# Two token mixers written as lists of steps in a two-layer trunk kernel

## The chip, the cores and the metric

The kernel runs on one core of one Trainium2 chip. The metric is device time in microseconds (us) of one execution; three runs of the kernel before are at hand, and one more execution under the profiler. The core's engines work side by side, each through its own queue in order: PE (TensorE, matmuls; PEld are its weight loads), DVE (VectorE), ACT (ScalarE), POOL (GpSimd) and SP (SyncE, which here issues most loads). PE writes its results into PSUM, where the kernel holds eight tiles of 128x512; the rest lives in SBUF.

## What is computed

A batch of one, 256 tokens, width 1024, two layers. Each layer is a half-step feed-forward block, a token mixer and a second half-step feed-forward block; every part has an RMS norm ahead of it, with shift, scale and gate from a conditioning vector `c`. Layer 0 mixes by MoBA attention (with 256 tokens a single causal block, with a relative-position bias), layer 1 by MLA.

```python
def swiglu(h, w_gate, w_up, w_down):
    return (jax.nn.silu(h @ w_gate) * (h @ w_up)) @ w_down
...
for layer in range(DEPTH):
    mods = c_act @ ada_w[layer] + ada_b[layer]
    sh1, sc1, g1, sh2, sc2, g2, sh3, sc3, g3 = jnp.split(mods, 9, axis=-1)
    h = modulate(rms_norm(x, norm_g[layer, 0]), sh1, sc1)
    x = x + 0.5 * g1[:, None, :] * swiglu(h, ffn_w_gate[layer, 0], ffn_w_up[layer, 0], ffn_w_down[layer, 0])
    h = modulate(rms_norm(x, norm_g[layer, 1]), sh2, sc2)
    mix = moba_attention(h, ...) if layer < N_A_LAYERS else mla_attention(h, ..., shared_k, shared_v, positions)
    x = x + g2[:, None, :] * mix
    h = modulate(rms_norm(x, norm_g[layer, 2]), sh3, sc3)
    x = x + 0.5 * g3[:, None, :] * swiglu(h, ffn_w_gate[layer, 1], ffn_w_up[layer, 1], ffn_w_down[layer, 1])
...
def mla_attention(h, w_dq, q_a_norm_g, w_uq, q_g, w_o, k, v, positions):
    q = (rms_norm(h @ w_dq, q_a_norm_g) @ w_uq).reshape(B, S, MLA_HEADS, MLA_QK)
    q = rms_norm(q, q_g)
    q = jnp.concatenate([q[..., :MLA_NOPE], rope(q[..., MLA_NOPE:], positions)], axis=-1)
    o = causal_block_attention(q, k, v, MLA_QK ** -0.5)
    return o.reshape(B, S, MLA_HEADS * MLA_V) @ w_o
```

All arrays are float32. There are 16 heads; in MoBA of width 64, in MLA 96 for queries and keys (64 and a rotated part of 32) and 64 for values. The feed-forward width is 2816.

## The kernel before

Tokens stand in two tiles of 128 (`t` 0 and 1). A float32 product is made of three matmuls: each operand is split into a rounded part `hi` (an ACT copy) and the rest `lo` (a DVE subtraction), and `mm3` (L393 to L397) sums hi x hi, hi x lo and lo x hi into one PSUM bank. Weights come by SP into `raw` tiles (three buffers) in the order in which `wsrcs` lists them, one ahead of their use; `split` makes their parts.

`ffn` (L506) runs four times. It takes the first 512 hidden columns tile by tile (32 triple products of 512 columns), then 18 blocks of 128 hidden rows with both token tiles side by side as a moving operand of 128x2x128 (16 triple products each, gate and up), then two halves of the down product, 22 blocks deep. In the second half tile 0 runs eight blocks ahead of tile 1, so that tile 0's residual (`ry`, `x`), norm and transposes can go on under tile 1's last eight blocks.

The conditioning vectors, 18 of width 1024, are made on DVE: `ada_vec` (L201) takes eight steps, each a 512 KB load into one of three `adaw` buffers and one accumulation into `acc` (one buffer), and then sums over partitions on PE, `adaps`: with transposes and DVE reductions for shifts and scales, with products by ones for gates, whose `acc` is split first. The steps are dealt out by a planner that counts an estimate of PE's time, `clock`: `pe(us)` adds to it, runs what has come due (`later`), and takes one step of the stream whenever `clock` has passed the next mark. The marks are set by `ada_pace(vectors, us)`, which spreads the steps still wanted over that many clock us, 172 for a feed-forward block (90 for the last); `ada_until(vectors)` takes what is left at once. `ffn` calls it after tile 0's last residual and ahead of tile 0's norm. What the planner emits is then put in order by a scheduler that weighs program order against its own estimate of when operands are ready; each engine's final order can be read from the built kernel.

```python
    def pe(us):
        clock[0] += us
        if busy[0]:
            return
        while pend and pend[0][0] <= clock[0]:
            run_next()
        while pace[0] and clock[0] >= pace[1]:
            pace[1] += pace[0]
            ada(1)
```

The mixers are planned by the same clock. `moba` (L817) projects queries and keys of four groups of four heads (`qk`) and values (`vals`); some microseconds of clock later (`T_WAIT`, `S_WAIT`, `PT_WAIT`, `AV_WAIT`) come the transposes `to_T` and the three parts of `attention` (L594): `scores` with the softmax, `transposes` of the weights, `av`. `mla` (L1006) does the same from two latents, normed and transposed by `lat_norm_T`. A query is scaled by its 1/rms (`head_rstd`: ACT square, DVE sums, POOL power) before it is rotated and transposed. `out_proj` (L679) follows, in two halves of the depth, with residual and norm after each tile.

## Time and profile before

| | us |
|---|---|
| runs: lowest, median, highest of 3 | 1061.85, 1062.43, 1064.68 |
| the profiled execution | 1067.16 |
| its span, first to last instruction | 1065.4 |

The profile's lines are read so: engine, operation, `out<-in` with the names of the program's tiles, partitions x elements, how often; then busy us, mean ns of one, and the engine's idle time ahead of them with what ended it. Stages by time: first block to 237 us, MoBA to 372, second block to 557, third to 756, MLA to 874, fourth to the end.

### The profile page before, as it was taken

How to read it: one execution, taken by the hardware profiler on the slowest of the kernel's cores; microseconds unless marked ns; L12 is line 12 of the kernel's file. 1: busy time of each engine (PE TensorE's matmuls, PEld its weight loads, DVE VectorE, ACT ScalarE, POOL GpSimd, SP SyncE). 2: the span in 40 equal slices, each digit the busy share in tenths (PEclk: the TensorE clock that was granted, in tenths of full speed). 3: DMA queues.
4: the chain of work that ended last, by engine and by line, in shares of the span. 5: the costliest groups of instructions: out<-in, count | busy, mean ns of one | idle time of the engine just before them, and what ended most of it. 6: DMA issues, size and time to landing. Idle time of an engine off the chain costs nothing.

```text
span 1065.4 us, 17278 instructions
## 1 busy us (share of the span) xinstructions
PE 1020.8 (96%) x6663; PEld 899.3 (84%) x6663; DVE 810.9 (76%) x1244; ACT 578.6 (54%) x1048; POOL 70.1 (7%) x119
## 2 busy tenths in 40 slices
PE   4999999998999999999999999999988899999998
PEld 2499999886778789999887999988766778999986
DVE  5999977886875789889688888867778758755642
ACT  4364545357675765545348544533868777545531
POOL 4001000002121000000000000000043200000000
PEclk9999999999999999999999999999999999999999
DMA  9999987996845479989897997986354337665450
GB/s 311 322 304 287 376 288 278 335 318 206 310 162 170 139 236 345 337 293 332 295 313 227 328 329 251 318 303 205 117 162 142 119 119 236 223 204 187 161 177 20
DMA packets 166934, 260.65 MB, mean 245 GB/s; under 512 B 8030, under 2 KB 110214, under 8 KB 166852
## 3 DMA queue, kind: packets, MB, share of 16 engines
q1 hardware_dynamic: 164496, 254.70, 70.3%
q0 software_dynamic: 976, 3.37, 1.0%
q10 hardware_dynamic: 1380, 1.49, 0.5%
q8 instruction: 52, 0.85, 0.3%
q14 instruction: 30, 0.25, 0.1%
HBM read 255.33 MB, written 4.19 MB: 244 GB/s over the span
## 4 chain that ended last, share of the span: by engine, by line
PE 77%; DVE 10%; ACT 4%; DMA 4%; POOL 3%; issue 3%; SPq 0%; DVEq 0%; ACTq 0%; POOLq 0%
PE mm L394 23%; PE mm L396 23%; PE mm L395 23%; DVE lo L196 3%; POOL hr L703 3%; DMA adaw<-in_ada_w_dram 2%; PE mm L198 2%; ACT hi L196 1%; DVE oh L722 1%; PE adaps L222 1%; PE at L666 1%; PE at L611 1%; DVE acc L211 1%; DMA raw<-in_ffn_w_gate_dram 1%; ACT y L196 1%
## 5 line engine op out<-in xcount | busy, mean ns | idle before, releaser
L196 DVE TENSOR_TENSOR lo<-raw,hi 128x1024 fp32r<-128x1024 f32 (+2 forms) x316 | 374.3, 1199 | 80.2 <-ACT hi L196 79.3
L196 ACT ACTIVATE hi<-raw 128x1024 fp32r<-128x1024 f32 (+2 forms) x316 | 324.1, 1040 | 171.5 <-PE mm L396 103.6
L394 PE MATMUL mm<-hh,hi 128*128 128x256 f32 x1152 | 328.6, 285 | 0.0
L396 PE MATMUL mm<-hh,lo 128*128 128x256 f32 x1152 | 326.7, 284 | 0.5 <-DVE lo L196 0.5
L395 PE MATMUL mm<-hl,hi 128*128 128x256 f32 x1152 | 326.5, 283 | 0.0
L395 PEld LDWEIGHTS mm<-hl,hi 128*128 128x128 f32 x1152 | 221.7, 192 | 0.6 <-issue 0.2
L396 PEld LDWEIGHTS mm<-hh,lo 128*128 128x128 f32 x1152 | 221.6, 192 | 0.7 <-DVE lo L196 0.7
L394 PEld LDWEIGHTS mm<-hh,hi 128*128 128x128 f32 x1152 | 221.7, 192 | 0.6 <-issue 0.2
L211 DVE SCALAR_TENSOR_TENSOR acc<-adaw,cact,acc 128x1024 f32<-128x1024 f32 x126 | 162.8, 1292 | 20.6 <-DMA adaw<-in_ada_w_dram 16.2
L394 PE MATMUL mm<-hi,gh 128*128 128x512 f32 x352 | 138.0, 392 | 0.0
L395 PE MATMUL mm<-lo,gh 128*128 128x512 f32 x352 | 137.0, 389 | 0.0
L396 PE MATMUL mm<-hi,gl 128*128 128x512 f32 x352 | 137.0, 389 | 0.0
L394 PE MATMUL mm<-hi,hh 128*128 128x512 f32 (+1 forms) x240 | 96.7, 404 | 5.0 <-ACT hh L196 5.0
L396 PE MATMUL mm<-hi,hl 128*128 128x512 f32 (+1 forms) x240 | 94.0, 392 | 1.5 <-DVE hl L196 1.4
L395 PE MATMUL mm<-lo,hh 128*128 128x512 f32 (+1 forms) x240 | 93.4, 390 | 0.0
L560 ACT ACTIVATE g<-mm 128x256 f32<-128x256 f32 x72 | 27.3, 379 | 94.5 <-PE mm L396 94.5
L396 PEld LDWEIGHTS mm<-hi,gl 128*128 128x128 f32 x352 | 66.1, 188 | 13.8
L394 PEld LDWEIGHTS mm<-hi,gh 128*128 128x128 f32 x352 | 66.1, 188 | 13.2
L395 PEld LDWEIGHTS mm<-lo,gh 128*128 128x128 f32 x352 | 66.1, 188 | 13.1
L196 ACT ACTIVATE gh<-g 128x256 fp32r<-128x256 f32 x72 | 29.9, 416 | 69.6 <-DVE g L561 69.6
L394 PEld LDWEIGHTS mm<-hi,hh 128*128 128x128 f32 x240 | 45.1, 188 | 16.1 <-ACT hh L196 7.8
L396 PEld LDWEIGHTS mm<-hi,hl 128*128 128x128 f32 x240 | 45.1, 188 | 13.2 <-DVE hl L196 4.5
(222 smaller groups left out, 1114.8 us busy)
## 6 DMA issues: line engine op xcount, KB each, us to landing
adaw<-in_ada_w_dram SPq DMA_DIRECT2D x144, 512.0 KB, 6.8
raw<-in_ffn_w_gate_dram SPq DMA_DIRECT2D x42, 1024.0 KB, 7.3
raw<-in_ffn_w_up_dram SPq DMA_DIRECT2D x42, 1024.0 KB, 6.9
raw<-in_ffn_w_down_dram SPq DMA_DIRECT2D x40, 1024.0 KB, 6.6
raw<-in_moba_w_qkv_dram SPq DMA_DIRECT2D x16, 512.0 KB, 5.0
adaw<-in_kv_ada_w_dram SPq DMA_DIRECT2D x16, 512.0 KB, 5.6
raw<-in_ffn_w_down_dram SPq DMA_DIRECT2D x8, 512.0 KB, 3.6
raw<-in_moba_w_qkv_dram SPq DMA_DIRECT2D x4, 1024.0 KB
```

The lines of the kernel that those rows point to most:

```text
L196: return fn(*args, **kw)
L198: chain[on] = fn(*args, **kw)
L211: nc.vector.scalar_tensor_tensor(acc, wt, cact[:, k:k + 1], bz if k == 0 else acc, op0=ALU.mult, op1=ALU.add)
L222: nc.tensor.transpose(kslice(pt, j), kslice(acc, 4 * hh + j), ident)
L394: nc.tensor.matmul(ps, lh, rh, start=start, stop=False)
L395: nc.tensor.matmul(ps, lh, rl, start=False, stop=False)
L396: nc.tensor.matmul(ps, ll, rh, start=False, stop=stop)
L560: nc.scalar.activation(g, ps[:, 0], AF.Silu)
L611: nc.tensor.matmul(ps3[:, i, :], qTs(e, t), kTs(e, nk), start=bias is not None, stop=bias is not None or i == len(es) - 1)
L666: nc.tensor.matmul(po[i * DH:(i + 1) * DH, pr, t, :], vs(e, kb), pT[t, e, kb], start=kb == 0, stop=kb == t)
L703: nc.gpsimd.tensor_tensor(r, v2, mhalf[:, :nh], op=ALU.pow)
L722: return fn(*args, **kw)
```

## The change

It writes both mixers as lists of steps. `in_steps` goes through a list and holds each step's matmuls behind the last matmul of the step before in PE's queue, so that within the mixers PE's order is that of the list. The letters: `d`, `e` the two latents, `l`, `c` their transposes, `q`, `k`, `v` the projections, `r`, `u`, `t` transposes of queries and keys, `s`, `p`, `a` scores, transposed weights and values, `o` output products of one tile and one pair of depths, `n` residual and norm of a tile.

In MLA the query is no longer scaled: an ACT copy takes it from PSUM, and its 1/rms scales the maximum and goes into the exponential as a scale per query. The key transposes leave PSUM by DVE in place of ACT. The causal mask is added after the scores and covers only the diagonal block. The output product is split into four pairs of depth for each tile, dealt out among the last attention steps and round the first tile's norm. `mm3` reports another estimate to the planner's clock. Smaller edits: the load order of MoBA's last two projections is swapped, some scratch tiles share a buffer, score tiles have six buffers for five and values three for two, a sum of the head norm is made in place.

```diff
+MOBA_ORDER = ("q00 q01 v00 t0 v010 s0 v011 q100 p0 q101 a0 q11 q20 t1 q210 s1 q211 q300 p1 q301 a1 t2 q310 s2 q311 "
+              "v200 p2 v201 t3 v210 s3 v211 o00 a2 p3 o10 a3 o01 o02 o03 n0 o11 o12 o13 n1").split()
+MLA_ORDER = ("d0 d1 l0 e0 l1 e1 c0 q00 q01 c1 k00 k01 r0 q10 q11 k10 u0 k11 r1 s0 q20 q21 u1 k20 k21 p0 r2 s1 a0 "
+             "q30 q31 u2 k30 k31 p1 r3 s2 a1 u3 o00 s3 o01 p2 o10 a2 p3 o02 a3 o11 o03 n0 o12 o13 n1").split()
...
-                    for g in (0, -1, 1, 2, -2, 3):
+                    for g in (0, -1, 1, 2, 3, -2):
...
-        nc.tensor.matmul(ps, ll, rh, start=False, stop=stop)
-        pe(3 * max(256, rh.shape[-1]) * 0.422e-3)
+        latest[0] = nc.tensor.matmul(ps, ll, rh, start=False, stop=stop)
+        pe(3e-3 * (rh.shape[-1] / 2.4 + 13.3))
+
+    latest = [None]
+    chained = [None]
+
+    def in_steps(order, fns):
+        for w in order:
+            with ExitStack() as es:
+                if chained[0]:
+                    es.enter_context(tc.issue_after(chained[0].ins))
+                latest[0] = None
+                fns[w[0]](*map(int, w[1:]))
+            chained[0] = latest[0] or chained[0]
...
-                if bias is None:
-                    nc.tensor.matmul(ps, ident_b, masks[t], start=True, stop=False)
...
+                if not bias:
+                    latest[0] = nc.tensor.matmul(ps3[:, :, t * P:], ident_b, mask[:, :len(es) * P]
+                                                 .rearrange("p (e k) -> p e k", k=P), start=False, stop=True)
...
+                    raw = small([P, 4], "mxr")[:, :n]
+                    nc.vector.tensor_reduce(raw, ps3, axis=AX.X, op=ALU.max, negate=True)
+                    nc.vector.tensor_tensor(mx, raw, rq(t)[:, es[0]:es[0] + n], op=ALU.mult)
...
-                                         bias=mxs[u][:, i:i + 1], scale=1.0 if bias is None else -1.0,
+                                         bias=mxs[u][:, i:i + 1], scale=-1.0 if bias else rq(t)[:, e:e + 1],
...
+        def products(t, j):
+            for half in range(2):
+                if (t, half) not in acc:
+                    acc[t, half] = mm_tile()
+                for k in (2 * j, 2 * j + 1):
...
+                    mm3(acc[t, half], *hk(oT[t], k), *pls[half, k], start=k == 0, stop=k == KD - 1)
...
-                    r = head_rstd(ap, pq_, GH * QK, QK)
-                    nc.vector.tensor_tensor(qn[:, t], heads(pq_), r[:, :, None].to_broadcast([P, GH, QK]), op=ALU.mult)
...
+                ps = proj(("q", g), t, qlT, QL // P, GH * QK)
+                nc.scalar.activation(qn[g][:, t], heads(ps), AF.Copy)
+                rq[g, t] = head_rstd(ap, ps, GH * QK, QK)
...
-                    nc.scalar.activation(dst[:, :, t * P:(t + 1) * P],
-                                         pt[:QK, :].rearrange("p (e q) -> p e q", q=P), AF.Copy, scale=gcol)
...
+                    if kind == "q":
+                        nc.scalar.activation(*ev, AF.Copy, scale=gcols[0])
+                    else:
+                        nc.vector.tensor_scalar(*ev, gcols[1], None, op0=ALU.mult)
```

## The prediction

> **What bounds the kernel now.** I read the page first, then busy time by stage, then single stretches in order of time.

> ```profile
> span 1065.4 us, 17278 instructions
> PE 1020.8 (96%) x6663; PEld 899.3 (84%) x6663; DVE 810.9 (76%) x1244; ACT 578.6 (54%) x1048; POOL 70.1 (7%) x119
> ```
> ```profile
> 50.00:237.00 187.00, 184.97 (x1462) 169.99 (x1461) 165.84 (x256) 93.29 (x166) 5.85 (x3) 0.99 0.91 311
> 237.00:256.00 19.00, 16.12 (x74) 11.81 (x74) 11.13 (x21) 16.60 (x38) 3.87 (x5) 1.00 0.49 173
> 256.00:363.50 107.50, 104.00 (x582) 86.12 (x581) 78.62 (x160) 67.55 (x135) 16.93 (x10) 1.00 0.63 213
> 363.50:372.00 8.50, 6.37 (x30) 4.33 (x29) 5.70 (x10) 7.88 (x22) 1.12 (x2) 1.00 0.38 125
> 372.00:557.00 185.00, 185.00 (x1243) 170.87 (x1242) 156.81 (x172) 93.42 (x135) 0.00 (x0) 1.00 0.88 305
> 756.00:771.00 15.00, 13.84 (x78) 11.49 (x77) 12.18 (x38) 14.33 (x41) 0.55 (x1) 1.00 0.38 115
> 771.00:867.00 96.00, 85.66 (x531) 69.35 (x531) 73.42 (x169) 66.29 (x164) 25.87 (x20) 1.00 0.44 141
> 867.00:874.00 7.00, 5.32 (x27) 3.89 (x26) 5.66 (x10) 6.58 (x18) 0.82 (x2) 1.00 0.41 126
> ```

> TensorE sets the time. The rows give a stretch, its length, then busy time of PE, PEld, DVE, ACT and POOL. In the second feed-forward block (372 to 557) PE never rests; whatever is taken off DVE or the DMA queues there gains nothing. What a better order can win is PE's rest in the mixers: 3.5 us inside MoBA (256 to 363.5), 10.3 inside MLA (771 to 867), and at their ends 2.9, 2.1, 1.2 and 1.7. The other side of the account is the seam between a feed-forward block and the next norm, where PE has only the rest of tile 1's products as cover.

> **The clock of the plan: the part that decides.** The change also rewrites what `mm3` adds to the planner's clock, from `max(256, n)` columns to `n`, with n the last dimension of the moving operand. For the gate and up products the operand is 128x2x128, so n is 128 while 256 columns move.

> ```profile
> 400.32 0.28 PE L394 MATMUL mm<-hh,hi 128*128 128x256 f32 x1
> 400.44 0.28 PE L395 MATMUL mm<-hl,hi 128*128 128x256 f32 x1
> ```

> Start to start they take 0.12 us, 0.36 for three; the clock was moved 0.324 and is now moved 3e-3 x (128/2.4 + 13.3) = 0.20. The conditioning stream (`ada`, one 512 KB load and one accumulation a step) is paced by that clock: its steps are spread over 172 clock us a block. Up to the call of `ada_until` a block runs 32 triple products of its first columns (not on the clock in the first block), 288 of gate and up, and 80 down products: 0.648 x 112 + 0.324 x 288 = 166 of 172 before, 0.68 x 112 + 0.20 x 288 = 134 now, or 78%; in the first block 112 of 172. The rest of the steps is issued in one go by `ada_until`, at the very end of the block. The order of instructions of the two builds bears this out: after tile 0's last residual is traced, 12, 10 and 8 steps are left at the ends of blocks one, two and three, where before it was 4, none and 1. Each time a whole vector of eight falls behind tile 0's last product. Its column sums (eight transposes, `adaps`) stand in PE's queue *ahead* of the next norm's transposes, so all that follows on PE waits for that vector, though the next norm doesn't use it.

> ```profile
> L211 DVE SCALAR_TENSOR_TENSOR acc<-adaw,cact,acc 128x1024 f32<-128x1024 f32 x126 | 162.8, 1292 | 20.6 <-DMA adaw<-in_ada_w_dram 16.2
> L196 DVE TENSOR_TENSOR lo<-raw,hi 128x1024 fp32r<-128x1024 f32 x300 | 361.5, 1220 | 75.5 <-ACT hi L196 74.7
> L495 DVE TENSOR_TENSOR ry<-mm,gate 128x512 f32<-128x512 f32 x24 | 16.5, 686 | 14.7 <-PE mm L396 14.2
> L496 DVE TENSOR_TENSOR x<-x,ry 128x512 f32<-128x512 f32 x24 | 16.5, 688 | 0.4
> L257 DVE TENSOR_REDUCE acol<-adaps 128x4 f32<-128x512 f32 x12 | 7.8, 684 | 0.8 <-PE adaps L222 0.8
> L196 ACT ACTIVATE y<-tr,m_cols 128x128 f32<-128x128 f32 x80 | 32.6, 457 | 0.2
> L196 ACT ACTIVATE hh<-y 128x256 fp32r<-128x256 f32 x40 | 16.7, 418 | 0.4 <-PE tr L442 0.3
> ```
> ```profile
> 232.37 0.68 DVE L495 TENSOR_TENSOR ry<-mm,gate 128x512 f32<-128x512 f32 x1
> 235.60 0.39 PE L395 MATMUL mm<-lo,gh 128*128 128x512 f32 x1
> 235.83 0.39 PE L396 MATMUL mm<-hi,gl 128*128 128x512 f32 x1
> 236.06 1.03 PE L222 MATMUL adaps<-ident,acc 128*128 128x128 f32 x8
> 236.85 0.48 PE L394 MATMUL mm<-hi,gh 128*128 128x512 f32 x1
> 240.93 0.50 PE L394 MATMUL mm<-hi,hh 128*128 128x512 f32 x1 [0.88 <-ACT hh L196]
> ...
> 554.81 0.68 DVE L495 TENSOR_TENSOR ry<-mm,gate 128x512 f32<-128x512 f32 x1
> 563.35 0.50 PE L394 MATMUL mm<-hi,hh 128*128 128x512 f32 x1 [0.86 <-ACT hh L196]
> ...
> 748.24 0.69 DVE L495 TENSOR_TENSOR ry<-mm,gate 128x512 f32<-128x512 f32 x1 [0.20 <-PE mm L396]
> 756.58 0.45 PE L394 MATMUL mm<-hi,hh 128*128 128x384 f32 x1 [0.47 <-ACT hh L196]
> ```

> Call T the start of tile 0's last residual. From T to the next stage's first product it took 8.56, 8.54 and 8.34 us. Now, from the DVE order of the changed build (each engine works its queue in order, as the rows above show):

> First seam, from T to the end of the vector: nine accumulations 9 x 1.29 = 11.6, the split of the gate sum 1.22, six weight splits 7.3, two residual pairs 2.75, three small ones 0.45 (0.15 each, estimated from their size): T + 23.3. Second seam: `acc` has one buffer, so the vector starts when PE has read the one before it: 18 products at 0.23 (235.60 to 235.83) and eight transposes 0.79 (236.06 to 236.85), T + 4.9; then eight accumulations 10.3, four splits 4.9, a residual pair 1.4, a reduce 0.7, a small one: T + 22.4. Third: T + 4.9, eight accumulations 10.3, splits of 288, 864 and 288 columns (by size 0.35, 1.03, 0.35), pair 1.4, reduce 0.7, 0.15: T + 19.2. Behind that on PE come 0.79 of column sums and a pair of transposes, 0.2, then 2 x 0.457 + 0.418 on ACT, together 2.3. First products: T + 25.6, 24.7, 21.5; extra 17.0, 16.2, 13.2, in sum 46.4.

> To it come the loads. There are three `adaw` buffers, so the fourth load is issued only after the first accumulation.

> ```profile
> DMA to landing us min/median/max: 3.5/6.6/9.2
> ```

> At 3.5 us every load lands before its accumulation is reached; at 6.6 the fourth and seventh are waited for, by my reckoning 2.5, 3.2 and 4.6 us in the three seams. Bounds 46.4 and 56.7; I take 51.5. What is queued behind the waiting instructions on DVE is the next norm's own splits, so nothing passes. On SP the leftover loads wait for their buffers ahead of later weight loads: in the first seam MoBA's value weights are among them, due only after 48 query products (10.9 us), so this costs nothing while those run.

> PE then rests about 15 us at each seam. The nearest row of such a rest is short:

> ```profile
> 90.95 1.63 PE L722 MATMUL tr<-tab,oh 128*128 128x64 bf16 x24 [1.56 <-DVE oh L722]
> ...
> 90.00:95.00 5.00, 4.05 (x37) 3.68 (x38) 5.00 (x13) 3.51 (x18) 0.00 (x0) 0.78 1.13 362
> 95.00:100.00 5.00, 5.00 (x40) 5.00 (x39) 4.87 (x9) 0.62 (x1) 3.23 (x1) 0.88 1.02 373
> ```

> After it the granted clock was 0.78 and 0.88 over two stretches of 5 us: 1.1 + 0.6 = 1.7 us of clock lost. At three seams 5.1; bounds 0 and twice that. Loss in all 56.6.

> **What the mixers win.** The orders written out put 24 products of 512 columns between a query group and its transposes, where before three stood.

> ```profile
> 291.76 0.38 PE L879 MATMUL tr<-ident,qn 128*128 128x128 f32 x2
> 293.45 0.77 PE L879 MATMUL tr<-ident,qn 128*128 128x128 f32 x5 [1.31 <-DVE qn L858]
> ```

> Three such waits make up most of MoBA's rest: gain 4 (0 to 6: a restart costs more than the bar leaves open). In MLA the query's own chain loses the wait for POOL and the scaling on DVE, eight times:

> ```profile
> L703 POOL TENSOR_TENSOR hr<-hv,mhalf 128x4 f32<-128x4 f32 x16 | 22.7, 1420 | 41.8 <-DVE hv L702 41.8
> L1085 DVE TENSOR_TENSOR qn<-mm,hr 128x384 f32<-128x384 f32 x8 | 4.5, 557 | 6.7 <-POOL hr L703 6.7
> L1066 ACT ACTIVATE kT<-tr,gck 96x512 f32<-96x512 f32 x8 | 5.3, 694 | 1.2 <-PE tr L1065 1.2
> L609 PE MATMUL at<-mask,ident_b 128*128 128x512 bf16 x12 | 4.6, 384 | 0.0
> ```

> An ACT copy of 384 columns takes its place (0.5, estimated between the 0.418 for 256 and the 0.694 for 512), and the key transposes' evacuation goes from ACT to DVE, 0.69 each. DVE was busy 73.4 of MLA's 96 us and gives 4.5, takes 5.5: it stays near its load, and three copies of 1/rms ride on the product of four columns. So I don't take all of the 10.3: 8 (0 to 13). The score buffers now hold 1/rms until the exponentials have read it, in eight slots; POOL's next results wait there, which keeps me off the full figure. Masks of 256 for 512 columns in eight of twelve: 8 x 0.11 = 0.9. Output products put round the norm lengthen the cover at the mixers' ends, of 2.1 + 1.7: 2.5. After the long wait at a seam DVE has the splits done that PE waited for in the rows 237:256 and 756:771: 2.5. In the first block DVE was full around 90 us and has fewer accumulations now: 2 of its 2.0 rest and 1.7 clock. Gain in all 19.9. Scratch tiles that now share buffers, the joined masks' set-up and the changed load order of MoBA's last two weights I put at nothing: their users lie a stage apart, and if one waits it is by a split, 1.2.

> PE's bar leaves 10.3 us of rest in MLA. [...]

> Sum: +51.5 + 5.1 - 19.9 = +36.7. On the profiled execution, 1067.16 us with its span of 1065.4, that is 1103.9; the median of the runs is 4.7 lower, 1062.43, so 1099.

> **Rivals.** *The seams cost only what is counted there twice, half.* Were the scheduled splits and residuals hidden behind load waits and the clock not cut, 3 x (10.3 - 2.0 of products) = 25 would be lost and 19.9 won: 1068 to 1080. Against it: the DVE order leaves no idle to hide them in. *The mixers hold more than PE's bars show.* At the second block's share of weight loads (170.87 of 185) MLA's 69.35 would fill 75.1 of its 96 us: 20.9 won in place of 8, 1086. For it speak the many switches between transposes and products, whose pauses a bar covers; against it DVE, busy 73.4 there. *Faster.* If the vectors left over were accumulated under the down products, because their loads come early, the seams cost nothing and 19.9 is won: 1043. It decides where the eight accumulations end before T + 7; that needs `acc` free and eight loads landed with three buffers, against the row of 3.5 us at least. *The queued matmuls don't help.* Waiting at the head of PE's queue, with ACT and DVE each near 75% in MLA, could leave the mixers as they are: +56.6 and 1119.

> **How the numbers follow.** Forecast (1085 to 1112) 0.62; queue without help 0.14; more in the mixers 0.08; half cost 0.08; faster 0.08, of which 0.02 within the bound. A measurement can tell 0.3%, 3.2 us, from no change. So slower 0.92, same 0.02, faster 0.06. The range: low end with 46.4, no clock lost, and gains of 30 (6 + 13 and the ends in full): +16; high end 56.7 + 10.2 less 5: +62. That is 1078 to 1124, which holds the forecast, the larger gain, and most of the queue without help.

> **What would show it.** Right: at three places, about 237, 570 and 780 us, PE rests 10 us or more, its first following instruction is `adaps`, released by DVE `acc`, and the granted clock dips behind each; four to eight accumulations stand in one run on DVE there. Fewer accumulations per us in gate and up stretches, PE still full there. MoBA's waits `tr<-ident,qn` on `qn` gone; MLA's stretch shorter by 5 to 10 us, DVE above 80% busy. Wrong: no rest at the seams, or rests under 5 us; MLA as long as before or longer.

## The result and the profile after

| | before | after |
|---|---|---|
| runs, us: lowest, median, highest | 1061.85, 1063.43, 1064.68 (4) | 1126.91, 1129.07, 1131.39 (4) |
| span of the profiled execution | 1065.4 | 1128.7 |

The changed kernel takes 1.0618 times as long (95% interval 1.0588 to 1.0649), 65.6 us more, where 36.7 were forecast and at most 62 allowed for. The direction was right, the size was not. From the page of the changed kernel: its span, its engines' busy time, the clock that TensorE was granted in 40 slices, and the rows of the accumulations and of the column sums:

```profile
span 1128.7 us, 17306 instructions
PE 1027.2 (91%) x6663; PEld 910.0 (81%) x6663; DVE 821.8 (73%) x1256; ACT 581.3 (52%) x1048; POOL 73.6 (7%) x117
PEclk9999999987999999999987999999798999999999
L214 DVE SCALAR_TENSOR_TENSOR acc<-adaw,cact,acc 128x1024 f32<-128x1024 f32 x126 | 163.0, 1294 | 28.0 <-DMA adaw<-in_ada_w_dram 23.0
...
L225 PE MATMUL adaps<-ident,acc 128*128 128x128 f32 x96 | 15.2, 311 | 52.2 <-DVE acc L214 52.2
```

PE has as many instructions as before and is busy 6.4 us longer, but its share falls from 96% to 91%. The last row holds most of the new rest: 52.2 us ahead of the column sums, all of it waiting for `acc` on DVE. The accumulations themselves stood idle for 28.0 us, 23.0 of them for loads, where it was 20.6 and 16.2. The clock is granted less in and just behind those places: 0.65 over 236 to 265 us, 0.59 over 582 to 607, 0.64 over 796.6 to 815.8.

To see where the rest of the time went, the execution is cut at points that both kernels have: the last product of a feed-forward block, the first product of the next stage, and, behind a mixer, the first two-token product of the feed-forward block (so the mixers' stretches hold its 32 triple products of 512 columns too). The rows give stretch, length, busy time of PE, PEld, DVE, ACT and POOL with instructions, then granted clock, share of the DMA engines and GB/s. First the seams and mixers of before, then of after:

```profile
239.20:240.90 1.70, 0.85 (x6) 0.50 (x4) 1.70 (x3) 1.70 (x6) 0.68 (x2) 1.00 0.96 339
240.90:392.10 151.20, 143.54 (x756) 116.17 (x757) 107.59 (x205) 104.31 (x214) 21.23 (x16) 1.00 0.58 194
561.70:563.40 1.70, 0.84 (x7) 0.51 (x5) 1.70 (x3) 1.70 (x6) 0.00 (x0) 1.00 0.52 172
755.20:756.60 1.40, 0.93 (x8) 0.57 (x6) 1.40 (x4) 1.08 (x4) 0.00 (x0) 1.00 0.57 170
756.60:895.90 139.30, 126.58 (x731) 102.29 (x732) 105.86 (x232) 105.33 (x253) 27.53 (x23) 1.00 0.43 139
```
```profile
241.30:265.10 23.80, 4.07 (x18) 3.27 (x16) 17.87 (x20) 7.67 (x14) 3.06 (x4) 0.57 0.91 306
265.10:413.90 148.80, 143.63 (x756) 117.61 (x757) 105.14 (x199) 102.30 (x211) 21.80 (x13) 0.99 0.59 197
582.20:605.20 23.00, 4.09 (x19) 3.29 (x17) 17.90 (x21) 7.67 (x15) 1.46 (x1) 0.59 0.92 313
796.60:815.80 19.20, 4.06 (x19) 3.32 (x17) 14.90 (x23) 2.72 (x8) 0.70 (x1) 0.64 0.75 240
815.80:959.20 143.40, 126.28 (x731) 106.64 (x732) 108.13 (x238) 104.80 (x250) 23.67 (x22) 0.96 0.38 122
```

The three seams were 1.7, 1.7 and 1.4 us and are 23.8, 23.0 and 19.2: 61.2 more, nearly the whole loss between the profiled executions (1128.7 - 1065.4 = 63.3). MoBA won 2.4. MLA, for which the largest gain was forecast, is 4.1 longer at a granted clock of 0.96. The remaining stretches, all feed-forward, differ by 2.1, -1.3, -0.4 and 0 us.

The second seam in order of time (start, length, engine, line, operation; in brackets the idle time ahead and what ended it):

```profile
575.62 0.69 DVE L512 TENSOR_TENSOR ry<-mm,gate 128x512 f32<-128x512 f32 x1 [1.53 <-PE mm L399]
...
582.08 1.28 DVE L214 SCALAR_TENSOR_TENSOR acc<-adaw,cact,bz 128x1024 f32<-128x1024 f32 x1
...
594.59 2.60 DVE L214 SCALAR_TENSOR_TENSOR acc<-adaw,cact,acc 128x1024 f32<-128x1024 f32 x2
599.84 1.28 DVE L214 SCALAR_TENSOR_TENSOR acc<-adaw,cact,acc 128x1024 f32<-128x1024 f32 x1 [2.66 <-DMA adaw<-in_kv_ada_w_dram]
...
601.18 1.97 PE L225 MATMUL adaps<-ident,acc 128*128 128x128 f32 x8 [18.58 <-DVE acc L214]
602.94 1.91 PE L459 MATMUL tr<-ident,y 128*128 128x128 f32 x8
605.18 0.80 PE L397 MATMUL mm<-hi,hh 128*128 128x512 f32 x1 [0.33 <-ACT hh L199]
```

Tile 0's last residual starts at 575.62, the leftover vector's first accumulation at 582.08. The last accumulation waits 2.66 us for its load, and PE rests 18.6 us until it is done. The norm's transposes stand behind the column sums, and all of it runs at half clock (0.50 over 600 to 606 us): eight column sums take 1.97 us, against 1.03 in the row at 236.06 of before, where the clock was 1.00.

In MLA the first transposes of the query's latent, as PE and DVE show them, and the clock on both sides of that rest:

```profile
826.78 0.34 PE L399 MATMUL mm<-hi,hl 128*128 128x384 f32 x1
831.93 0.90 PE L1013 MATMUL tr<-ident,ly 128*128 128x128 f32 x3 [4.81 <-DVE ly L1007]
832.48 0.59 PE L397 MATMUL mm<-hi,hkv 128*128 128x288 f32 x1
```
```profile
826.00:832.00 6.00, 1.03 (x5) 0.72 (x6) 5.56 (x19) 4.39 (x11) 2.38 (x2) 1.00 0.56 169
832.00:836.00 4.00, 4.00 (x20) 4.00 (x21) 3.33 (x5) 0.49 (x1) 0.00 (x0) 0.58 0.52 144
```

The list has `l0` ahead of `e0`. Its transposes wait 4.8 us for the normed latent `ly`, which DVE (busy 5.56 of these 6 us) makes behind the key latent's modulation, and `e0`'s products are held behind them. After the rest the clock stands at half for most of four us (0.58 over 832 to 836; by its record from 831.96 to 835.37).

### The profile page after: what moved, and what is told of

It reads as the page before. It is cut to its first block, busy times and chain, and to the rows that moved or that the text cites. A ratio compares the mean times of both kernels' runs of the same rounds, so it can differ in the third digit from the quotient of the medians.

```text
span 1128.7 us, 17306 instructions
## 1 busy us (share of the span) xinstructions
PE 1027.2 (91%) x6663; PEld 910.0 (81%) x6663; DVE 821.8 (73%) x1256; ACT 581.3 (52%) x1048; POOL 73.6 (7%) x117
## 4 chain that ended last, share of the span: by engine, by line
PE 68%; DVE 12%; DMA 8%; ACT 5%; issue 4%; SPq 2%; POOL 1%; DVEq 0%; ACTq 0%; POOLq 0%
PE mm L397 21%; PE mm L399 21%; PE mm L398 21%; DMA adaw<-in_ada_w_dram 5%; DVE lo L199 3%; DVE acc L214 3%; DMA adaw<-in_kv_ada_w_dram 2%; SPq L201 2%; ACT hi L199 1%; DMA raw<-in_ffn_w_gate_dram 1%; DVE oh L742 1%; PE adaps L225 1%; ACT s L654 1%; PE at L681 1%; ACT y L199 1%
## 5 line engine op out<-in xcount | busy, mean ns | idle before, releaser
L199 ACT ACTIVATE hi<-raw 128x1024 fp32r<-128x1024 f32 (+2 forms) x316 | 326.3, 1042 | 170.2 <-PE mm L399 103.5
L578 DVE TENSOR_TENSOR g<-mm,g 128x256 f32<-128x256 f32 x72 | 30.2, 419 | 50.3 <-ACT g L577 50.2
L225 PE MATMUL adaps<-ident,acc 128*128 128x128 f32 x96 | 15.2, 311 | 52.2 <-DVE acc L214 52.2
```

The costliest lines, as they stand in the source:

```text
L199: return fn(*args, **kw)
L225: nc.tensor.transpose(kslice(pt, j), kslice(acc, 4 * hh + j), ident)
L578: nc.vector.tensor_tensor(g, ps[:, 1], g, op=ALU.mult)
```

## The experiments

Twelve kernels, each timed beside runs of the kernel before on the same chip (whose medians were 1063.4 to 1066.3 us). MLA's length is that of the stretch above, in one profiled execution of each kernel.

| kernel | median, us | over before (95% interval) | MLA, us |
|---|---|---|---|
| changed | 1129.1 | 1.0618 (1.0588 to 1.0649) | 143.4 |
| changed, all columns counted | 1086.5 | 1.0214 (1.0194 to 1.0234) | 146.6 |
| changed, old estimate | 1074.1 | 1.0097 (1.0080 to 1.0113) | 145.8 |
| before, new estimate | 1122.6 | 1.0549 (1.0533 to 1.0565) | 140.4 |
| changed, leftover after the norm | 1126.4 | 1.0585 (1.0569 to 1.0601) | 158.8 |
| old estimate, not queued | 1060.8 | 0.9958 (0.9937 to 0.9978) | 132.5 |
| old estimate, latents' order | 1069.7 | 1.0038 (1.0021 to 1.0056) | 139.4 |
| old estimate, query scaled | 1090.6 | 1.0232 (1.0206 to 1.0257) | 162.6 |
| changed, late column sums | 1104.3 | 1.0363 (1.0336 to 1.0390) | 146.7 |
| old estimate, not queued, query scaled | 1070.7 | 1.0049 (1.0030 to 1.0067) | 141.4 |
| old estimate, rests filled | 1073.8 | 1.0075 (1.0052 to 1.0097) | 143.5 |
| changed, not queued | 1116.6 | 1.0483 (1.0462 to 1.0505) | 133.2 |
| all columns counted, not queued | 1071.1 | 1.0054 (1.0031 to 1.0077) | 133.3 |

### The estimate: three kernels

```diff
-        pe(3e-3 * (rh.shape[-1] / 2.4 + 13.3))
+        pe(3e-3 * (math.prod(rh.shape[1:]) / 2.4 + 13.3))
```

> The changed kernel with one edit: mm3 tells the planner's clock all columns of the moving operand (256 for 128x2x128, so 0.36 us a triple product), not the last dimension alone. Theory A (the 65.6 us over before are the three seams, 52.7 in the changed profile, and about 7 of clock behind them; the mixers as written neither win nor lose much): 1129 - 52.7 - 7 = about 1069, range 1060 to 1080, no column sum waited for at 237, 570, 780. Theory B (the late seam at the third block's end also causes what MLA lost, because weights and splits come late behind it): the mixers' gains show and the time is 1040 to 1056, below before. Theory C (the pace isn't the cause): 1110 or more.

```diff
-        pe(3e-3 * (rh.shape[-1] / 2.4 + 13.3))
+        pe(3 * max(256, rh.shape[-1]) * 0.422e-3)
```

> The changed kernel with the old estimate in mm3, 3 x max(256, n) x 0.422 ns, so that the conditioning stream is dealt out as before. What is left are the step lists, the 1/rms in the exponential and the output products round the norm. Theory A: within 5 us of the run with all columns counted, 1060 to 1080. Theory B: 1040 to 1056. Theory C: 1110 or more. If this one is more than 8 us faster or slower than the run with all columns, the exact pace matters beyond whether whole vectors are left over.

The third is the kernel before with the new line, the reverse of the second:

> The kernel before with one edit: the new estimate in mm3 (last dimension only). Nothing of the mixers changed but what their planner's clock decides. Theory A: 1063 + 53 + 7 = about 1122, range 1110 to 1132, with the three rests of PE ahead of the column sums. Theory B (the losses in MLA belong to the step lists meeting a late seam): 1110 to 1118, because the old mixers are planned by the same clock and shift. Theory C: 1060 to 1070.

The seams' stretches of that third kernel, in windows like those above:

```profile
237.00:261.00 24.00, 3.68 (x18) 3.06 (x16) 18.13 (x20) 7.64 (x14) 3.06 (x4) 0.64 0.94 330
576.90:600.50 23.60, 4.11 (x18) 3.29 (x17) 18.00 (x21) 7.60 (x15) 1.59 (x2) 0.58 0.89 305
791.50:810.70 19.20, 4.00 (x19) 3.34 (x17) 14.91 (x23) 2.77 (x9) 0.70 (x1) 0.64 0.72 240
```

The one line in the old kernel makes the seams of the changed one, and 1122.6 us were measured for 1122 forecast by theory A; with the line put back, the changed kernel is at 1074.1. So the estimate makes the seams, and theory C falls. Theory B falls too: without the seams the mixers as written don't win, they are 1% slower than before. The first of the three was missed: the true count was to give 1069 and gave 1086.5. It has no rest over 0.2 us ahead of these column sums, but at the second block's end one of 5.7 us ahead of the norm's own transposes:

```profile
571.38 0.69 PE L459 MATMUL tr<-ident,y 128*128 128x128 f32 x2 [5.69 <-ACT y L454]
```

### The leftover steps taken later

```diff
-                    ada_until(ada_to)
+                    pace[0] = None
                     after(0)
...
             after(1)
+            ada_until(ada_to)
```

> The changed kernel with its estimate kept, but the leftover steps of the conditioning stream taken after the block's second norm is planned, not between tile 0's residual and its norm. The same 12, 10 and 8 steps are left over. Theory A (their place ahead of the norm's transposes in PE's queue makes the price): the rests of 14 to 20 us go, DVE still spends 10.3 us a seam on them beside the mixers' first products: 1070 to 1095. Rival (the DVE work and the loads themselves set the time, wherever they are put): 1110 or more.

1126.4: the rival's number, and theory A as stated fell. The column sums, in order of time, at the three places:

```profile
269.71 1.97 PE L225 MATMUL adaps<-ident,acc 128*128 128x128 f32 x8 [13.99 <-DVE acc L214]
...
612.45 1.97 PE L225 MATMUL adaps<-ident,acc 128*128 128x128 f32 x8 [8.02 <-DVE acc L214]
...
818.97 1.97 PE L225 MATMUL adaps<-ident,acc 128*128 128x128 f32 x8 [14.80 <-DVE acc L214]
```

The rests did not go but moved: PE waits 14.0, 8.0 and 14.8 us for `acc` in the first products of the next stage. That is 36.8 us for 52.2, but the stages that now hold these waits became longer by more than them (MoBA 174.5 us for 148.8, the third block 207.2 for 191.4, MLA 158.8 for 143.4). The planner puts a vector's sums 3 us of its clock behind the vector's last step, wherever that is planned, and eight accumulations alone are 10.3 us of DVE. That suggested the next kernel.

### The leftover vector's column sums planned later

```diff
-        later(3.0, sums if rows else col_sums)
+        later(sums_wait[0], sums if rows else col_sums)
...
         while ada_done[0] < vectors * KD:
+            sums_wait[0] = 16.0 if ada_done[0] >= (vectors - 1) * KD else 3.0
             ada(1)
+        sums_wait[0] = 3.0
```

> The changed kernel with its estimate kept and the leftover steps taken where they were, but the sums over partitions of the last leftover vector planned 16 us of clock behind its last step, in place of 3. (Taking the leftover steps behind the norm had put them 3 us into the next stage, and PE rested there as long.) Theory A, mended (the price is that the planner takes a vector for done 3 us after its last step is issued): the rests at the seams shrink from 19.6, 18.7 and 14.4 to under 5, with 10 us of DVE a seam left beside the mixers' first products: 1075 to 1095. Rival (the eight accumulations and loads hold up DVE's splits, and with them PE, wherever the sums stand): 1110 or more.

1104.3, between the two. Its three seams, in windows, and the third one's end in order of time:

```profile
242.80:244.40 1.60, 0.90 (x7) 0.54 (x5) 1.60 (x3) 1.60 (x6) 0.60 (x1) 1.00 0.99 369
...
579.40:581.20 1.80, 0.82 (x6) 0.49 (x4) 0.70 (x1) 1.80 (x6) 0.00 (x0) 1.00 1.15 352
774.40:788.20 13.80, 0.99 (x6) 0.45 (x4) 11.10 (x15) 2.39 (x6) 0.70 (x1) 0.61 0.74 240
```
```profile
786.42 0.42 DVE L465 COPY xT<-tr 128x256 f32<-128x256 f32 x1
...
788.24 0.69 PE L400 MATMUL mm<-hi,hh 128*128 128x384 f32 x1 [12.64 <-ACT hh L200]
```

Two seams are back at 1.6 and 1.8 us: there the sums' place was the price of the rest. At the third, PE waits 12.6 us for `hh`, because before it DVE has to copy the transposed tile (`xT`), and that copy stands behind seven of the same eight accumulations in DVE's queue. MoBA pays part of it back (163.7 us against 148.8), with the accumulations beside its first products.

### The lists without the queue

```diff
             with ExitStack() as es:
-                if chained[0]:
-                    es.enter_context(tc.issue_after(chained[0].ins))
                 latest[0] = None
```

> The run with the old estimate (1074.1, MLA 145.8 us from its first product to the fourth block's first two-tile product, against 139.3 before), with one edit: the lists are still the order of the program, but no step's matmuls are held behind the preceding step's, so the scheduler may pass a step that waits. Theory D (a step that stands at the head of PE's queue and waits over 1.7 us is what MLA lost, for each such wait is followed by 3.4 us at half clock, 6.8 us in all): 1062 to 1067, at most one half-clock stretch in MLA. Theory E (DVE's and ACT's load in MLA sets its length, in whatever order): 1071 to 1077.

The two mixers with the queue (old estimate) and without it:

```profile
239.00:388.80 149.80, 144.54 (x756) 117.23 (x757) 104.32 (x203) 104.13 (x214) 21.17 (x16) 0.99 0.56 191
755.10:900.90 145.80, 129.03 (x727) 107.78 (x732) 110.14 (x244) 107.36 (x254) 23.04 (x23) 0.95 0.40 132
```
```profile
241.50:389.60 148.10, 143.02 (x756) 116.00 (x757) 104.44 (x203) 104.04 (x214) 21.24 (x16) 1.00 0.57 193
755.50:888.00 132.50, 125.99 (x726) 103.29 (x731) 107.60 (x244) 106.20 (x254) 26.83 (x23) 0.99 0.44 145
```

1060.8, the fastest of all and 0.4% faster than before. DVE and ACT have the same work in MLA (244 and 254 instructions), so their load does not set its length, and theory E falls. The waits of PE in MLA (what waits on what: us in total, times, longest), with the queue and without:

```profile
PE tr L1013 <- DVE ly L1007: 4.6, 2, 4.1
PE tr L1112 <- ACT s L654: 3.0, 2, 2.1
PE tr L1112 <- ACT hi L199: 2.2, 1, 2.2
```
```profile
PE tr L1110 <- ACT s L652: 1.4, 2, 0.7
...
PE tr L1011 <- DVE ly L1005: 0.3, 1, 0.3
```

With the queue PE stands at transposes whose input is late, or that wait for the exponentials. Without it they are passed. The clock takes its share: summed over the records of the granted clock, MLA lost up to 6.8 us to stretches at half clock with the queue (four of 3.41 us; a granted clock of 0.95 in the row above), 1.7 without (0.99), and none before (1.00). So of the 13.3 us that the queue costs here, at most 5.1 are clock, as PE may have rested in a part of those stretches. By the rows above, PE is busy 3.0 us longer with the queue and rests 10.3 us more.

The same edit in the changed kernel with its own estimate shows whether the two losses add:

> The changed kernel with its own estimate kept, lists not queued. If the two losses add up (seams with the clock behind them; the queue in the mixers), 1129.1 - (1074.1 - 1060.8) = 1116, range 1111 to 1120, with the three rests as long as in the changed kernel. If the queue's losses in the mixers come from the late seams, less is won: 1121 or more.

1116.6 for 1116. The seams stand at 24.4, 23.5 and 19.2 us, and the mixers at 145.6 and 133.2: the losses are separate.

### One step of the list

```diff
-MLA_ORDER = ("d0 d1 l0 e0 l1 e1 c0 q00 ...
+MLA_ORDER = ("d0 d1 e0 l0 e1 l1 c0 q00 ...
```

> The run with the old estimate, with one edit of MLA's list: each latent's transposes stand one product later (d0 d1 e0 l0 e1 l1 for d0 d1 l0 e0 l1 e1), which puts 3.2 us of products ahead of the transposes on which PE rested 4.3 us. Theory D: that rest falls to about 1 and its half-clock stretch goes, 3.2 + 1.7 = 5 us won, 1069. Theory E: the rest moves to the next step that needs DVE, 1072 to 1075.

1069.7 for 1069; MLA is at 139.4 us, as before the change, with two half-clock stretches where four were (a granted clock of 0.98 for 0.95). Two steps moved by one place are worth as much as all that MLA had lost (6.4 us of this stretch, 4.3 in the medians).

### The 1/rms back on the query

```diff
-                nc.scalar.activation(qn[g][:, t], heads(ps), AF.Copy)
-                rq[g, t] = head_rstd(ap, ps, GH * QK, QK)
+                r = head_rstd(ap, ps, GH * QK, QK)
+                nc.vector.tensor_tensor(qn[g][:, t], heads(ps), r[:, :, None].to_broadcast([P, GH, QK]), op=ALU.mult)
...
-                    raw = small([P, 4], "mxr")[:, :n]
-                    nc.vector.tensor_reduce(raw, ps3, axis=AX.X, op=ALU.max, negate=True)
-                    nc.vector.tensor_tensor(mx, raw, rq(t)[:, es[0]:es[0] + n], op=ALU.mult)
+                    nc.vector.tensor_reduce(mx, ps3, axis=AX.X, op=ALU.max, negate=True)
...
-                                         bias=mxs[u][:, i:i + 1], scale=-1.0 if bias else rq(t)[:, e:e + 1],
+                                         bias=mxs[u][:, i:i + 1], scale=-1.0 if bias else 1.0,
```

> The run with the old estimate, with the 1/rms taken out of the exponential again: the query is scaled by it on DVE straight out of PSUM, ahead of the rotation (no ACT copy, no product with the maximum, scale 1). Theory D: the chain from query to transposes gets the wait for POOL back (1.4 us and the queue round it, for each group), so the rests ahead of the query transposes grow by 1 to 3 us: 1075 to 1082. Theory E (it is load): 4.5 us of DVE come and some 2 go, ACT gives 4: 1072 to 1078. If it is faster than 1072, the 1/rms in the exponential was itself part of the loss.

1090.6, more than either theory expected. PE's largest wait in MLA there:

```profile
PE tr L1110 <- DVE qn L994: 19.9, 4, 5.8
```

Four times the queue stands for the scaled and rotated query, 5 us each. The same edit without the queue:

> Lists not queued, old estimate (1060.8, MLA 132.5 us), with the query scaled by its 1/rms on DVE ahead of the rotation again. In the queued lists that edit cost 16.5 us, as five rests of 4.3 to 6.0 us ahead of transposes with half clock behind each. Theory D (a late chain costs what stands queued behind it): with the queue gone the scheduler passes the waiting transposes, and the edit costs 1 to 5 us, 1062 to 1066. Theory F (the wait for POOL is the price itself): 10 us or more, 1071 to 1077.

1070.7 for 1060.8: 9.9 us, nearer to theory F than to D. Without the queue the edit still costs 8.9 us of MLA (141.4 for 132.5). So the 1/rms in the exponential is worth some 9 us of MLA when the order is free, and 16.8 (162.6 less 145.8) when it is not. It is also all that MLA wins: with the query scaled as before, the lists without the queue are 2.1 us longer there than the kernel before (141.4 for 139.3), so no run shows MLA's new order as a gain by itself.

### PE kept at work in the rests

```diff
-MLA_ORDER = ("d0 d1 l0 e0 ...
+MLA_ORDER = ("d0 d1 w20 l0 e0 ...
...
+            def warm(n):
+                ps = mm_tile()
+                for i in range(n):
+                    latest[0] = nc.tensor.matmul(ps, ident_b, mask, start=True, stop=True)
...
```

with `w11` ahead of `r2` and of `u3` too. In the trace of before such a product, 128x512 in bf16, takes 0.22 us from its start to the next one's.

> The run with the old estimate, queued, with PE kept at work in three of MLA's rests: 20, 11 and 11 matmuls of the identity with the mask (512 columns of bf16, 0.21 us each, 4.3, 2.3 and 2.3 us), whose results nobody reads, ahead of the transposes for which it rested 4.3, 2.4 and 2.3 us. They take no work away. Theory D (the half clock follows PE's rest): the three half-clock stretches behind them go though the waits stay, 3 x 1.7 = 5 us won, less up to 2 where a filler outlasts the wait: 1069 to 1072, MLA 140.7 to 143. Rival (the half clock goes with something else in these places, the switch of operations or the load): the stretches stay, 1074 to 1077.

```profile
760.70:904.20 143.50, 131.44 (x773) 106.40 (x774) 109.63 (x244) 107.16 (x254) 26.16 (x23) 1.00 0.41 134
```

All four half-clock stretches of MLA are gone (granted clock 1.00 for 0.95), those behind rests that were not filled among them. But MLA is only 2.3 us shorter, and the total is 1073.8 for 1074.1. PE got on faster and then met other late operands:

```profile
PE tr L1112 <- DVE qn L996: 6.6, 3, 2.4
```

That wait was 1.1 us in the kernel without the fillers. So filling PE's rests took the half clock away here, as theory D has it. But its 6.8 us could not be had back by themselves: with the queue, what the clock gave was waited for elsewhere. Nor did every such rest bring half clock: PE still waits four times here, 1.6 to 2.5 us long, and none is followed by it (granted clock 1.00).

### The true count without the queue

The first experiment's line together with the edit that takes the queue away.

> Lists not queued and all columns counted in the estimate (0.36 us a gate or up triple product, as measured). With the queue in place the true estimate was 12.4 us slower than the old one of 0.324 (1086.5 against 1074.1), 11.6 of it in the first two blocks (243.2 and 177.1 us against 237.3 and 171.3). If the pace does that by itself (the conditioning steps fall on DVE and the queues at a worse time), the gap stays: 1071 to 1076. If it came from the queue or from the moment in which half-clock stretches fall, it is gone: 1059 to 1065.

1071.1: the gap stays, 10.3 us, so it is the pace. Between the two profiled executions, which lie further apart (spans of 1072.9 and 1057.6 us), 9.6 us of it are in the second block's stretch:

```profile
394.70:574.50 179.80, 171.33 (x1174) 158.92 (x1173) 149.22 (x165) 80.06 (x114) 1.46 (x1) 0.99 0.91 315
```

179.8 us where the kernel with the old estimate has 170.2, with a rest of 6 us ahead of the norm's transposes as in the first experiment. Why the steps fall worse there is not settled: the traces show tile 0's chain from residual to norm late behind accumulations and weight splits on DVE, but no run took these out one by one.

## Why the prediction was wrong, by its own steps

**The clock of the plan: right.** Three rests ahead of column sums, released by `acc`, at 241, 582 and 797 us, 14 to 19 us long. From the start of tile 0's last residual to the next stage's first product it was 30.6, 29.6 and 25.8 us for a forecast of 25.6, 24.7 and 21.5, so the extra was 60.5 in place of 46.4. Of the 14.1 between, 8.4 lie ahead of the column sums, and DVE's waits for loads there come to the same sum: 5.7 for `adaw` (0.43 in the first seam, 2.66 in the second, in the row at 599.84, 2.58 in the third), for which 5.1 were taken, and 2.77 in the first seam for `moba_q_g`, a small load that the forecast did not count and that stood ahead of accumulations in DVE's queue. The other 5.7 lie behind the start of the column sums, where 5.1 was taken for the clock. Taken together, 56.6 was forecast and 60.5 came. The kernel before with the new line alone, 58.0 us slower, confirms the term.

**What the mixers win: wrong by some 20 us, and the main part of the miss.** Here 19.9 us of gain were forecast, 17.9 of them in the mixers. The profiled stretches outside the seams came out 2.1 longer together, the mixers 1.7. The step that failed is the one that took PE's rest in MoBA (4) and MLA (8) for time that lists would win. It counted the products that the list puts ahead of a wait, and not what stands behind the wait. A list that is kept in PE's queue turns each late operand into a stop of all PE's work, and the list of MLA has such places: `l0` (4.8 us in the changed kernel), then transposes behind scores and weights. With the old estimate and the lists unqueued MLA wins 6.8 us (139.3 to 132.5) and MoBA 3.1, and the queue took 13.3 and 1.7 from them. With the changed kernel's own estimate the queue costs 10.2 and 3.2 (143.4 for 133.2, 148.8 for 145.6), which is 13.4 of the 19.6 us between forecast and result in the mixers. The 8 for the query's chain in MLA was fair, at 8.9 measured without the queue, and so was the 4 for MoBA, at 3.1 and 5.6 with all else that changed there. The other 6.2 us stay open; beside the 8 and the 4, 5.9 were forecast for masks, entries and exits, which no run took out one by one. The rival "the queued matmuls don't help" had this mechanism, but priced it at no gain (1119), not at a loss; it was given 0.14.

**The clock behind short rests: left out.** 1.7 us were counted at each seam and nothing inside the mixers. MLA of the changed kernel spent 10.2 us at half clock (3.41 from 831.96 and 6.83 from 849.03; 0.96 over the stretch), which is up to 5.1 us lost, where before there was no such stretch.

**Masks, exits, entries, first block (7.9 together): not seen one by one.** The first block's stretch was 239.2 before and 241.3 after, but the other kernels gave 237.0 to 243.2, with no order by their pace, so the 2 us forecast there can't be told from chance. MoBA with the changed kernel's estimate and no queue was 5.6 shorter than before (145.6), so entries and exits may have brought something there; no run isolates it.

**The rest:** "DVE above 80% busy" in MLA did not come (108.13 of 143.40, 75%). Whether the slots of the 1/rms held POOL up was not tried. The rivals with half the seams' cost and with a faster kernel fell, as the seams cost in full. "More in the mixers" fell for this kernel as well. The estimate behind it, PE's headroom by the share of weight loads, is neither borne out nor refuted: with free lists MLA won 6.8 us of the 20.9 that this share left open, nearer to the 8 that the bar gave. That PE's bar covers pauses, which the prediction gives for this rival, is seen in the rows of before: bars of 0.28 us start 0.12 us apart, at 400.32. In MLA the product at 787.21 and the transposes at 787.79 start 0.58 us apart, 0.41 more than the 0.17 between the products ahead of them, and the bar shows 0.24 of that as idle.

## What to carry over

When an edit changes a number that a planner paces by, work out where its backlog is flushed and who stands in the queues behind it, before anything else: one line cost 58 of the 65.6 us here, and the accurate count was slower than the old rough one, so a pace is a tuned value and has to be measured again. Write an order as the order in which work is offered, and force it in an engine's queue only where each step's operands are surely there: with the old estimate, the same mixers made the kernel 0.4% faster than before when the scheduler could pass a late step, and 1% slower when it could not.

## What the runs showed of the hardware

In the fourteen traces the starts of successive matmuls, less the median spacing behind a matmul of that shape, give PE's rests. In the changed kernel a rest of 2.1 us ended at 393.83 and half clock came at 395.05, for 3.41 us; one of 4.98 us ended at 831.93, with half clock from 831.96; one of 2.35 us ended at 877.63, and the clock stayed at 1.00. Counted over all fourteen is whether a stretch at half clock (3.41 us or a multiple) began in the rest or within 4.5 us of its end. For rests that begin at full clock, with no other rest of 1 us or more within 4.5 us on either side, it did with 5 of 94 rests of 1.0 to 1.6 us, with 29 of 48 of 1.6 to 2.4, with 4 of 9 of 2.4 to 3 and with all 15 of 3 to 7. These counts say what followed a rest; that the rest is the cause was tried only in MLA, where PE kept at work in three rests left no stretch at half clock (granted clock 1.00 for 0.95).
